# Gate and up projections with the weights standing and both halves of the activations in one moving operand; attention scores over zero-padded keys

## The chip, the cores and the metric

One Trainium2 chip, one core. The metric is the device time of one execution in microseconds (us); the shown time is a median of three runs. The profile is one execution on the same core.

## The reference

Two decoder layers over 256 tokens of width 1024, in fp32. Each layer is a feed-forward half step (FFN), a mixer (a state-space head group beside a windowed attention with 16 heads of 64) and a second FFN:

```python
def swiglu(x, w_gate, w_up, w_down):
    return (jax.nn.silu(x @ w_gate) * (x @ w_up)) @ w_down
...
for i in range(DEPTH):
    x = x + 0.5 * swiglu(rms_norm(x, ffn1_norm[i]), ffn1_w_gate[i], ffn1_w_up[i], ffn1_w_down[i])
    h = rms_norm(x, mix_norm[i])
    proj = h @ w_in[i]
...
    q = rms_norm(q.reshape(b, s, ATT_HEADS, ATT_HEAD_DIM), q_norm[i])
    k = rms_norm(k.reshape(b, s, ATT_HEADS, ATT_HEAD_DIM), k_norm[i])
    y_att = dilated_attention(q, k, v).reshape(b, s, ATT_WIDTH)
    x = x + jnp.concatenate([y_ssd, y_att], axis=-1) @ w_out[i]
    x = x + 0.5 * swiglu(rms_norm(x, ffn2_norm[i]), ffn2_w_gate[i], ffn2_w_up[i], ffn2_w_down[i])
```

Gate and up are 1024 x 2816 each, down is 2816 x 1024. The scores of a head are q times k over 64 values, with masks that are laid over them.

## The kernel before

A product of fp32 operands is made of three products of fp32r operands: each operand is split into a high part (a rounded copy, by ScalarE) and a low part (the operand less the copy, by VectorE), and `mm3` (L243) adds high x high, high x low and low x high in PSUM. Weights come from memory in halves of 128 x 1024, four staging buffers deep; `Stream.pump` (L161, L163) splits each half into one of nine slots (five of `hp`, four borrowed from `wk`), `take` hands a half to the matmuls and `done` gives its slot back. `tick()` stands after each group of matmuls: it lets the stream split what has a free slot and moves the spawned generators (transposes, heads and the like) one step, so that they are laid between the groups. Instructions run in order on each engine.

The normalised activations are held transposed, features on partitions, as a high tile and a low tile of 8 x 256 (`xT_tiles`).

In an FFN (`ffn`) the 2816 columns of gate and up go in 11 steps of 256 columns each. A step makes two PSUM tiles (one for each 128 tokens) of 512 columns, 256 of gate and 256 of up: the activations stand in the array (128 x 128) and the weights move (512 columns). That is 8 feature tiles x 2 token tiles x 3 = 48 matmuls of 512 columns, in eight groups of six. `gated` (L404, L405) then takes Silu of the gate's columns on ScalarE and multiplies by the up's columns on VectorE. The product has tokens on partitions, and the down projection wants features there: `rest` waits four ticks, transposes the four 128 x 128 blocks on TensorE (L399) and splits the result out of PSUM (L209, L210). The first step has its own loop (`unit_first`), since the second token tile is normalised late. The pool `ps` has four PSUM banks for all large products; the down projection (`project_out`) holds all four (`acc`).

In the mixer, `unit_ch` is a product with the weights standing and 256 activation columns moving, three loads and three matmuls for each pair of tiles (`pc`). For attention, `qk_norm_T` transposes q and k and writes each, 128 x 512 at a time, on ScalarE (L674); two heads share the 128 partitions. `head_pair` makes the scores of a head by two fp32 matmuls over its 64 partitions (256 and 128 columns; L689, L690, the profile shows each as two records), one head on the lower and one on the upper half of the array. Batches of four head pairs follow the q and k blocks that they need.

Of the kernel before, what the change touches and what calls it, by code (L numbers as in the profile page):

```python
# [50 lines left out]
def tile_hybrid_trunk(ctx: ExitStack, tc: tile.TileContext, x, w_ffn_in, w_ffn_down, w_z, w_dtz,  # L51
# [188 lines left out]
    def tok(t):  # L240
        return slice(t * 128, (t + 1) * 128)
# [19 lines left out]
            guard["act"], guard["vec"] = urgent(split)(xT[0][:, 4 * b:4 * b + 4, tok(t)], xT[1][:, 4 * b:4 * b + 4, tok(t)], p)  # L261

    def xT_tiles():
        return (big.tile([128, KT, 256], F32R, tag="xTh", name="xTh"),
                big.tile([128, KT, 256], F32R, tag="xTl", name="xTl"))

    @urgent
    def normed(t, wB, acc=None, scale=None):
# [22 lines left out]
    def mm_pair(name, n):  # L291

        return [ps.tile([128, 512], F32, tag="mm", name=f"{name}{i}")[:, :n] for i in range(2)]
# [28 lines left out]
    def unit_ch(xT, o):  # L322

        for a in range(2):
            hf = st.take()
            for i in range(2):
# [6 lines left out]
                    st.done(hf)  # L333
                tick()

    def project_out(nk, yT, tail, scale, norm, need=None):

        wB = None  # L340
        acc = [mm_pair(f"acc{t}", 512) for t in range(2)]

        def step(k, t, b, hf):
            n = slice(b * 512, (b + 1) * 512)
            yh, yl = [a[:, 0, tok(t)] for a in yT(k)]
            mm3(acc[t][b], yh, yl, hf[0][:, n], hf[1][:, n], k == 0, k == nk - 1)

        for k in range(0, nk - tail, 2):
            hf = [st.take(), st.take()] if k + 1 < nk - tail else [st.take()]
            if need:  # L350
                until(need(k + len(hf) - 1))
            for t in range(2):
                for i, h in enumerate(hf):
                    for b in range(2):
                        step(k + i, t, b, h)
                    if t:
                        st.done(h)
                    tick()
            if wB is None and k >= nk // 2 and norm is not None:
                wB = norm_weight(*norm)  # L360
        late = [(k, st.take()) for k in range(nk - tail, nk)]
        if need:
            until(need(nk - 1))
        st.hold = HOLD and norm is not None
        for b in range(2):
            for i, (k, h) in enumerate(late):
                step(k, 0, b, h)
                if i % 2:
                    tick()
        xT = xT_tiles() if wB is not None else None  # L370
        xn = normed(0, wB, acc, scale)
        for b in range(2):
            for i, (k, h) in enumerate(late):
                if b and i == tail - TR_POS and xT:
                    transpose_norm(0, xn, xT)
                step(k, 1, b, h)
                if b:
                    st.done(h)
                if i % 2:
                    tick()  # L380
        xn = normed(1, wB, acc, scale)
        st.hold = False
        return xT, xn


    def ffn(layer, f, xT, xn, norm, tail):
        hA = [big.tile([128, 16, 256], F32R, tag=f"yA{i}", name=f"hA{i}") for i in range(2)]
        hB = [big.tile([128, FT - 16, 256], F32R, tag=f"yB{i}", name=f"hB{i}") for i in range(2)]

        def hT(k, n=1):  # L390
            return [a[:, k:k + n, :] for a in hA] if k < 16 else [b[:, k - 16:k - 16 + n, :] for b in hB]

        def rest(j, h):

            yield 4
            p = pt.tile([128, 2, 256], F32, tag="tr", name="tr")
            for i in range(2):
                for t in range(2):
                    pe.transpose(p[:, i, tok(t)], h[:, t, i * 128:(i + 1) * 128], ident)  # L399
            split(*hT(2 * j, 2), p)  # L400

        def gated(p, sg, h, t):

            act.activation(sg[:, t, :], p[:, 0:256], AF.Silu)  # L404
            vec.tensor_tensor(h[:, t, :], sg[:, t, :], p[:, 256:512], op=OP.mult)  # L405

        for j in range(FF // 256):
            sg = wk.tile([128, 2, 256], F32, tag="t2", name="sg", bufs=5)
            h = wk.tile([128, 2, 256], F32, tag="t2", name="hh", bufs=5)
            p = mm_pair("pgu", 512)  # L410
            if j == 0:
                halves = [st.take() for _ in range(4)]
                for t in range(2):
                    if t:
                        transpose_norm(1, xn, xT)
                        if layer == 0 and f == 0:
                            small_params()
                    unit_first(512, xT, t, halves, p[t])
                    gated(p[t], sg, h, t)
            else:  # L420
                unit_tok(512, 2, xT, p)
                for t in range(2):
                    gated(p[t], sg, h, t)
            spawn(rest(j, h))
        return project_out(FT, hT, tail, 0.5, norm)


    def mixer(layer, xT, xn, norm, tail):
# [221 lines left out]


        qT = wk.tile([128, 8, 256], F32, tag="e0", name="qT", bufs=1)
        kT = wk.tile([128, 8, 256], F32, tag="e1", name="kT", bufs=1)
        vt = [wk.tile([128, D], F32, tag="xn", name=f"vt{t}") for t in range(2)]

        def qk_norm_T(which, b, pp, dst):
            ss = sm.tile([128, 2, 8], F32, tag="qss", name="qss")
            for t in range(2):
                sq = wk.tile([128, 8, E], F32, tag="t2", name="sq", bufs=5)
                act.activation(sq.rearrange("p h e -> p (h e)"), pp[t], AF.Square, scale=1.0 / 8)  # L660
                vec.tensor_reduce(ss[:, t, :], sq, axis=AX.X, op=OP.add)
            rr = rsqrt(ss, [128, 2, 8])
            qn = []
            for t in range(2):
                q = wk.tile([128, 8, E], F32, tag="t2", name="qn", bufs=5)
                vec.tensor_tensor(q, pp[t].rearrange("p (h e) -> p h e", e=E),
                                  rr[:, t, :, None].to_broadcast([128, 8, E]), op=OP.mult)
                qn.append(q.rearrange("p h e -> p (h e)"))
            yield 3
            for t in range(2):  # L670
                p = pt.tile([128, 4, 128], F32, tag="tr", name="tr")
                for i in range(4):
                    pe.transpose(p[:, i, :], qn[t][:, i * 128:(i + 1) * 128], ident)
                act.activation(dst[:, 4 * b:4 * b + 4, tok(t)], p, AF.Copy, scale=qkw[:, layer, which:which + 1])  # L674
            events.add(f"qk{which}{b}")

        RNG = (slice(0, 256), slice(256, 384))
# [1 line left out]
        def head_pair(pr):  # L679
# [4 lines left out]
            yield 1  # L684
            scs = []
            for i in range(2):
                o = slice(64 * i, 64 * i + 64)
                p = pt.tile([128, 384], F32, tag="s", name="psc")
                pe.matmul(p[:, 0:256], qT[o, pr, 128:256], kT[o, pr, :], start=True, stop=True)  # L689
                pe.matmul(p[:, 256:384], qT[o, pr, 0:128], kT[o, pr, 0:128], start=True, stop=True)  # L690
                sc = wk.tile([128, 384], F32, tag="sc", name="sc", bufs=4)
                nm = sm.tile([128, 2], F32, tag="nm", name="nm", bufs=4)
                den = sm.tile([128, 2], F32, tag="den", name="den", bufs=4)
                for j, c in enumerate(RNG):
                    vec.tensor_tensor_reduce(sc[:, c], p[:, c], amask[:, c], scale=-1.0, scalar=3e38,
                                             op0=OP.add, op1=OP.min, accum_out=nm[:, j:j + 1])
                for j, c in enumerate(RNG):
                    act.activation(sc[:, c], sc[:, c], AF.Exp, bias=nm[:, j:j + 1], scale=-1.0,
                                   accum_out=den[:, j:j + 1])
                vec.reciprocal(den, den)  # L700
                for j, c in enumerate(RNG):
                    vec.tensor_scalar(sc[:, c], sc[:, c], den[:, j:j + 1], None, op0=OP.mult)
                scs.append(sc)
                yield PAIR_LAG[i]
# [27 lines left out]
        for b, which in QKV_ORDER:  # L732
            pp = mm_pair("pq", 512)
            unit_tok(512, 2, xT, pp)
            if which < 2:
                spawn(qk_norm_T(which, b, pp, (qT, kT)[which]))
            else:
                for t in range(2):
                    act.copy(vt[t][:, 512 * b:512 * b + 512], pp[t])
                events.add(f"v{b}")  # L740
# [34 lines left out]
def _layout(inp):  # L775
# [2 lines left out]
    r = {"x": a["x"]}  # L778
    ffn_in = []
    for f in (1, 2):  # L780
        gu = [a[f"ffn{f}_w_{n}"].reshape(DEPTH, D, FF // 256, 256) for n in ("gate", "up")]
        ffn_in.append(_pack(np.stack(gu, axis=3).reshape(DEPTH, D, 2 * FF), 4, 512).transpose(0, 2, 1, 3, 4))
    r["w_ffn_in"] = np.stack(ffn_in, axis=1)
    r["w_ffn_down"] = np.stack([_pack(a[f"ffn{f}_w_down"], 2, 1024)[:, :, 0] for f in (1, 2)], axis=1)
    w = a["w_in"]
# [54 lines left out]
```

## Time and profile before

| what | value |
|---|---|
| median of three runs | 1246.6 us (1245.03 to 1246.91) |
| the profiled execution: time | 1244.8 us |
| its span, first to last instruction | 1242.9 us |
| granted TensorE clock, mean | 1.000 |
| TensorE matmul busy | 1228.6 us |
| VectorE busy | 784.7 us |
| ScalarE busy | 673.0 us |

The busy time of an engine is the time in which at least one of its instructions runs. The records of matmuls overlap each other, so that their mean duration is longer than the distance from one to the next. The chain is the work that ended last, followed back from the end; its pieces stand in order of time, with start and length, and their lengths add up.

### The profile page before, as it was taken

How to read it: one execution, taken by the hardware profiler on the slowest of the kernel's cores; microseconds unless marked ns; L12 is line 12 of the kernel's file. 1: busy time of each engine (PE TensorE's matmuls, PEld its weight loads, DVE VectorE, ACT ScalarE, POOL GpSimd, SP SyncE). 2: the span in 40 equal slices, each digit the busy share in tenths (PEclk: the TensorE clock that was granted, in tenths of full speed). 3: DMA queues.
4: the chain of work that ended last, by engine and by line, in shares of the span. 5: the costliest groups of instructions: out<-in, count | busy, mean ns of one | idle time of the engine just before them, and what ended most of it. 6: DMA issues, size and time to landing. Idle time of an engine off the chain costs nothing.

```text
span 1242.9 us, 16699 instructions
## 1 busy us (share of the span) xinstructions
PE 1228.6 (99%) x6176; PEld 1019.3 (82%) x6176; DVE 784.7 (63%) x1392; ACT 673.0 (54%) x1094; POOL 5.3 (0%) x13
## 2 busy tenths in 40 slices
PE   6999999999999999999999999999999999999998
PEld 5888888998777788888878888889987778888887
DVE  6655546897786576555466554478887865755541
ACT  5544434777866455444355443466778663644430
POOL 0000000000000000000000000000000000000000
PEclk9999999999999999999999999999999999999999
DMA  8755552654334557555447554645533443765550
GB/s 281 261 186 186 171 203 104 208 181 138 119 105 137 167 180 237 188 180 181 169 163 245 186 187 152 206 139 190 180 123 101 134 138 117 249 208 184 188 171 34
DMA packets 59409, 213.56 MB, mean 172 GB/s; under 512 B 6848, under 2 KB 7104, under 8 KB 59328
## 3 DMA queue, kind: packets, MB, share of 16 engines
q1 hardware_dynamic: 58176, 208.76, 49.7%
q0 software_dynamic: 1008, 3.67, 0.9%
q8 instruction: 49, 0.80, 0.3%
q14 instruction: 32, 0.26, 0.1%
q10 hardware_dynamic: 144, 0.07, 0.0%
HBM read 211.42 MB, written 1.05 MB: 171 GB/s over the span
## 4 chain that ended last, share of the span: by engine, by line
PE 97%; DVE 1%; DMA 1%; ACT 0%; issue 0%; SPq 0%; ACTq 0%
PE pgu L246 13%; PE pgu L245 13%; PE pgu L247 13%; PE acc L245 9%; PE acc L247 9%; PE acc L246 9%; PE pq L245 4%; PE pq L246 4%; PE pq L247 4%; PE pc L247 2%; PE pc L245 2%; PE pc L246 2%; PE psc L689 2%; PE tr L399 2%; PE pz L245 1%; PE pz L246 1%
## 5 line engine op out<-in xcount | busy, mean ns | idle before, releaser
L163 DVE TENSOR_TENSOR wl<-w,wh 128x1024 fp32r<-128x1024 f32 x268 | 327.6, 1224 | 191.6 <-ACT wh L161 189.0
L161 ACT CAST wh<-w 128x1024 fp32r<-128x1024 f32 x268 | 280.6, 1051 | 238.5 <-PE pgu L247 85.1
L163 DVE TENSOR_TENSOR we<-w,we 128x1024 fp32r<-128x1024 f32 x124 | 151.4, 1225 | 128.9 <-ACT we L161 127.6
L161 ACT CAST we<-w 128x1024 fp32r<-128x1024 f32 x124 | 130.2, 1053 | 136.5 <-PE pgu L247 68.9
L245 PE MATMUL pgu<-wh,xTh 128*128 128x512 f32 x392 | 156.8, 400 | 0.8 <-ACT xTh L209 0.8
L246 PE MATMUL pgu<-wl,xTh 128*128 128x512 f32 x392 | 154.6, 394 | 0.6 <-DVE wl L163 0.6
L247 PE MATMUL pgu<-wh,xTl 128*128 128x512 f32 x392 | 154.0, 394 | 0.0
L245 PE MATMUL pgu<-we,xTh 128*128 128x512 f32 x312 | 123.1, 395 | 0.0
L246 PE MATMUL pgu<-we,xTh 128*128 128x512 f32 x312 | 121.8, 390 | 0.0
L247 PE MATMUL pgu<-we,xTl 128*128 128x512 f32 x312 | 121.3, 390 | 0.0
L245 PEld LDWEIGHTS pgu<-wh,xTh 128*128 128x128 f32 x392 | 74.4, 190 | 17.0 <-ACT xTh L209 1.9
L246 PEld LDWEIGHTS pgu<-wl,xTh 128*128 128x128 f32 x392 | 74.5, 190 | 16.6 <-DVE wl L163 1.8
L247 PEld LDWEIGHTS pgu<-wh,xTl 128*128 128x128 f32 x392 | 74.4, 190 | 16.0 <-DVE xTl L210 0.3
L245 PE MATMUL pq<-wh,xTh 128*128 128x512 f32 x192 | 80.1, 417 | 0.0
L247 PE MATMUL pq<-wh,xTl 128*128 128x512 f32 x192 | 78.4, 408 | 0.0
L246 PE MATMUL pq<-wl,xTh 128*128 128x512 f32 x192 | 78.0, 406 | 0.0
L245 PE MATMUL pc<-xTh,wh 128*128 128x256 f32 x256 | 72.9, 285 | 0.0
L247 PE MATMUL pc<-xTh,wl 128*128 128x256 f32 x256 | 72.4, 283 | 0.0
L246 PE MATMUL pc<-xTl,wh 128*128 128x256 f32 x256 | 72.4, 283 | 0.0
L247 PEld LDWEIGHTS pgu<-we,xTl 128*128 128x128 f32 x312 | 58.5, 188 | 12.3
L246 PEld LDWEIGHTS pgu<-we,xTh 128*128 128x128 f32 x312 | 58.6, 188 | 12.1 <-DVE we L163 0.4
L245 PEld LDWEIGHTS pgu<-we,xTh 128*128 128x128 f32 x312 | 58.6, 188 | 11.9 <-ACT xTh L209 0.3
(189 smaller groups left out, 2222.2 us busy)
## 6 DMA issues: line engine op xcount, KB each, us to landing
w<-in_w_ffn_in_dram SPq DMA_DIRECT2D x176, 512.0 KB, 4.6
w<-in_w_ffn_down_dram SPq DMA_DIRECT2D x88, 512.0 KB, 3.7
w<-in_w_qkv_dram SPq DMA_DIRECT2D x48, 512.0 KB, 3.6
w<-in_w_xbc_dram SPq DMA_DIRECT2D x32, 512.0 KB, 4.4
w<-in_w_out_dram SPq DMA_DIRECT2D x32, 512.0 KB, 3.7
w<-in_w_z_dram SPq DMA_DIRECT2D x12, 512.0 KB, 4.7
nw<-in_norms_dram POOLq DMA_DIRECT2D x7, 512.0 KB, 4.2
w<-in_w_dtz_dram SPq DMA_DIRECT2D x4, 544.0 KB, 5.0
```

Of the source, the lines that this page charges most:

```text
L161: act.copy(h, src)
L163: vec.tensor_tensor(l, src, h.bitcast(F32), op=OP.subtract)
L245: pe.matmul(o, ah, bh, start=first, stop=False)
L246: pe.matmul(o, ah, bl, start=False, stop=False)
L247: pe.matmul(o, al, bh, start=False, stop=last)
L399: pe.transpose(p[:, i, tok(t)], h[:, t, i * 128:(i + 1) * 128], ident)
L689: pe.matmul(p[:, 0:256], qT[o, pr, 128:256], kT[o, pr, :], start=True, stop=True)
```

## The change

The steps 1 to 10 of each FFN hold the weights still. A step makes gate first (`pg`, two banks of 512 columns, one for each 128 features), then up (`pu`): for each weight tile one matmul of the high weights with the activations' high and low parts side by side (512 columns), and one of the low weights with the high activations (256 columns, into the first half of the bank). The two halves of a bank are added outside TensorE: ScalarE copies the second half out, VectorE adds the first. The product then has its features on partitions already, and is split straight into the down projection's operand. Step 0 stays as it was, with its transposes. The high and low activations lie in one tile, and the weights of steps 1 to 10 are laid out in memory in pieces of gate and of up.

The keys are kept twice as wide, each head's with zeros in the other head's 64 partitions: GpSimd sets the zeros once in each mixer, ScalarE writes k in two pieces of 64 partitions, and the scores are taken over all 128 partitions.

```diff
     def xT_tiles():
-        return (big.tile([128, KT, 256], F32R, tag="xTh", name="xTh"),
-                big.tile([128, KT, 256], F32R, tag="xTl", name="xTl"))
+        both = big.tile([128, KT, 2, 256], F32R, tag="xT", name="xT")
+        return both[:, :, 0, :], both[:, :, 1, :], both
...
+    def unit_ch_wide(xT, o):
+        for a in range(2):
+            hf = st.take()
+            for i in range(2):
+                for k in range(4):
+                    c = slice(k * 256 + 128 * i, k * 256 + 128 * i + 128)
+                    kk = 4 * a + k
+                    def wide(stop):
+                        pe.matmul(o[i], hf[0][:, c], xT[2][:, kk].rearrange("p s n -> p (s n)"),
+                                  start=kk == 0, stop=stop)
+                    if kk < KT - 1:
+                        wide(False)
+                    pe.matmul(o[i][:, 0:256], hf[1][:, c], xT[0][:, kk, :], start=False, stop=False)
+                    if kk == KT - 1:
+                        wide(True)
+                if i:
+                    st.done(hf)
+                tick()
...
-        def rest(j, h):
+        def turn(j, h):
...
+        def rest(j, h):
+            yield 1
+            split(*hT(2 * j, 2), h)
+
+        def halves_added(name, p):
+            o = wk.tile([128, 2, 256], F32, tag="t2", name=name, bufs=5)
+            for i in range(2):
+                act.copy(o[:, i, :], p[i][:, 256:512])
+                vec.tensor_tensor(o[:, i, :], p[i][:, 0:256], o[:, i, :], op=OP.add)
+            return o
...
+        spawn(turn(0, h))
+        for j in range(1, FF // 256):
+            pg, pu = mm_pair("pg", 512), mm_pair("pu", 512)
+            unit_ch_wide(xT, pg)
+            sg = halves_added("sg", pg)
+            act.activation(sg, sg, AF.Silu)
+            unit_ch_wide(xT, pu)
+            h = halves_added("hh", pu)
+            vec.tensor_tensor(h, sg, h, op=OP.mult)
             spawn(rest(j, h))
...
-        kT = wk.tile([128, 8, 256], F32, tag="e1", name="kT", bufs=1)
+        kz = wk.tile([128, 4, 2, 256], F32, tag="e1", name="kz", bufs=1)
+        pool.memset(kz[64:128, :, 0, :], 0.0)
+        pool.memset(kz[0:64, :, 1, :], 0.0)
...
-                act.activation(dst[:, 4 * b:4 * b + 4, tok(t)], p, AF.Copy, scale=qkw[:, layer, which:which + 1])
+                w = qkw[:, layer, which:which + 1]
+                if which:
+                    for i in range(2):
+                        o = slice(64 * i, 64 * i + 64)
+                        act.activation(kz[o, :, i, tok(t)], p[o], AF.Copy, scale=w[o])
+                else:
+                    act.activation(qT[:, 4 * b:4 * b + 4, tok(t)], p, AF.Copy, scale=w)
...
-                o = slice(64 * i, 64 * i + 64)
                 p = pt.tile([128, 384], F32, tag="s", name="psc")
-                pe.matmul(p[:, 0:256], qT[o, pr, 128:256], kT[o, pr, :], start=True, stop=True)
-                pe.matmul(p[:, 256:384], qT[o, pr, 0:128], kT[o, pr, 0:128], start=True, stop=True)
+                pe.matmul(p[:, 0:256], qT[:, pr, 128:256], kz[:, pr % 4, i, :], start=True, stop=True)
+                pe.matmul(p[:, 256:384], qT[:, pr, 0:128], kz[:, pr % 4, i, 0:128], start=True, stop=True)
```

## Rows read from the trace of the kernel before

**Rows 1.** The page, busy us, share of the span and instructions of each engine.
```profile
PE 1228.6 (99%) x6176; PEld 1019.3 (82%) x6176; DVE 784.7 (63%) x1392; ACT 673.0 (54%) x1094; POOL 5.3 (0%) x13
```
**Rows 2.** The page, shares of the chain that ended last, by engine.
```profile
PE 97%; DVE 1%; DMA 1%; ACT 0%; issue 0%; SPq 0%; ACTq 0%
```
**Rows 3.** Busy time by stretch, in steps of one FFN, 60 to 148 us.
```profile
core 0: us, PE busy (x) PEld busy (x) DVE busy (x) ACT busy (x) POOL busy (x), PEclk, DMA share, GB/s
60.00:148.00 88.00, 88.00 (x403) 72.91 (x402) 47.87 (x54) 42.48 (x55) 0.00 (x0) 1.00 0.54 185
```
**Rows 4.** The chain in order of time, one step of gate and up: start, us, what.
```profile
80.52 0.44 PE tr L399 x4
80.96 0.24 PE pgu L245
...
91.88 0.44 PE tr L399 x4
```
**Rows 5.** The page, costliest groups: count | busy us, mean ns | idle before.
```profile
L245 PE MATMUL pgu<-wh,xTh 128*128 128x512 f32 x392 | 156.8, 400 | 0.8 <-ACT xTh L209 0.8
```
**Rows 6.** The chain, weights standing, 256 columns moving: first and last of 67 pieces.
```profile
231.98 0.12 PE pc L245
...
239.90 0.12 PE pc L245
```
**Rows 7.** The chain at one head's scores, and the two matmuls behind.
```profile
385.32 0.63 PE psc L689 x2
385.94 0.22 PE psc L690 x2
386.17 0.43 PE acc L245
386.59 0.23 PE acc L246
```
**Rows 8.** The chain where two heads' scores stand together: first piece, and the matmul behind.
```profile
334.21 0.73 PE psc L689 x3
...
335.41 0.43 PE pq L245
```
**Rows 9.** The chain at fp32 matmuls over all 128 partitions, between fp32r ones.
```profile
286.54 0.43 PE pst L553 x2
286.97 0.23 PE pq L247
...
289.04 0.24 PE pcb L580 x2
...
298.21 0.84 PE py L595 x8
299.05 0.49 PE po L600 x2
```
**Rows 10.** Groups of instructions by line and shape, ScalarE and VectorE.
```profile
L674 ACT ACTIVATE kT<-tr,qkw 128x512 f32<-128x512 f32 x8 | 5.2, 680 | 0.0
L555 ACT COPY xB<-pst 128x256 f32<-128x256 f32 x8 | 3.0, 371 | 3.0 <-PE pst L553 3.0
...
L405 DVE TENSOR_TENSOR hh<-sg,pgu 128x256 f32<-128x256 f32 x88 | 36.1, 414 | 0.0
```
**Rows 11.** VectorE in order of time around a step's end in mid-FFN.
```profile
97.55 1.23 DVE L163 TENSOR_TENSOR wl<-w,wh 128x1024 fp32r<-128x1024 f32 x1 [1.17 <-ACT wh L161]
98.69 0.41 DVE L405 TENSOR_TENSOR hh<-sg,pgu 128x256 f32<-128x256 f32 x1
```
**Rows 12.** The chain near the third FFN's start: the transposes of its step 0.
```profile
647.35 0.44 PE tr L399 x4
```
**Rows 13.** VectorE in order of time: the two multiplications of that FFN's step 1.
```profile
656.41 0.75 DVE L405 TENSOR_TENSOR hh<-sg,pgu 128x256 f32<-128x256 f32 x2
```
**Rows 14.** Weight loads in order of time, scores of the second four pairs.
```profile
378.78 0.29 PEld L689 LDWEIGHTS psc<-kT,qT 64*128 64x128 f32 x2 [0.36 <-ACT kT L674]
```

More of the change, by code (lines that the diff above doesn't have):

```diff
@@ L405, in gated @@
             vec.tensor_tensor(h[:, t, :], sg[:, t, :], p[:, 256:512], op=OP.mult)
[L407 to L423, printed above, removed]
+        def rest(j, h):
[7 more added lines that the diff above has]
+            return o
+        sg = wk.tile([128, 2, 256], F32, tag="t2", name="sg", bufs=5)
+        h = wk.tile([128, 2, 256], F32, tag="t2", name="hh", bufs=5)
+        p = mm_pair("pgu", 512)
+        halves = [st.take() for _ in range(4)]
+        for t in range(2):
+            if t:
+                transpose_norm(1, xn, xT)
+                if layer == 0 and f == 0:
+                    small_params()
+            unit_first(512, xT, t, halves, p[t])
+            gated(p[t], sg, h, t)
+        spawn(turn(0, h))
[7 more added lines that the diff above has]
+            vec.tensor_tensor(h, sg, h, op=OP.mult)
             spawn(rest(j, h))
@@ L652, in mixer, with qk_norm_T @@
         qT = wk.tile([128, 8, 256], F32, tag="e0", name="qT", bufs=1)
-        kT = wk.tile([128, 8, 256], F32, tag="e1", name="kT", bufs=1)
+        kz = wk.tile([128, 4, 2, 256], F32, tag="e1", name="kz", bufs=1)
+        pool.memset(kz[64:128, :, 0, :], 0.0)
+        pool.memset(kz[0:64, :, 1, :], 0.0)
         vt = [wk.tile([128, D], F32, tag="xn", name=f"vt{t}") for t in range(2)]
-        def qk_norm_T(which, b, pp, dst):
+        def qk_norm_T(which, b, pp):
             ss = sm.tile([128, 2, 8], F32, tag="qss", name="qss")
@@ L735, in mixer @@
             if which < 2:
-                spawn(qk_norm_T(which, b, pp, (qT, kT)[which]))
+                spawn(qk_norm_T(which, b, pp))
             else:
@@ L780, in _layout @@
     for f in (1, 2):
-        gu = [a[f"ffn{f}_w_{n}"].reshape(DEPTH, D, FF // 256, 256) for n in ("gate", "up")]
-        ffn_in.append(_pack(np.stack(gu, axis=3).reshape(DEPTH, D, 2 * FF), 4, 512).transpose(0, 2, 1, 3, 4))
+        gu = [a[f"ffn{f}_w_{n}"] for n in ("gate", "up")]
+        first = _pack(np.concatenate([w[:, :, 0:256] for w in gu], axis=2), 4, 512).transpose(0, 2, 1, 3, 4)
+        rest = np.stack([_pack(w[:, :, 256:], 8, 256)[:, 0] for w in gu], axis=2)
+        ffn_in.append(np.concatenate([first, rest], axis=1))
     r["w_ffn_in"] = np.stack(ffn_in, axis=1)
```

## The prediction, on record before the result

> **What bounds the kernel now.** I read the busy times first [rows 1], then the chain by engine [rows 2]: TensorE is busy for 1228.6 of 1242.9 us and holds 97% of the chain. The stretch in the middle of an FFN [rows 3] says the same where the change lands: TensorE 88.00 of 88.00 us at a granted clock of 1.00 (the 2.4 GHz level), VectorE 54%, ScalarE 48%. So time comes out only by shortening TensorE's own sequence, and goes in wherever TensorE must wait for ScalarE, VectorE or a PSUM bank. The third view is the chain in order of time, which gives the distance from one matmul to the next; the recorded 400 ns of a 512-column matmul [rows 5] overlap their neighbours' and price nothing.
>
> **Gate and up.** One step runs from one set of transposes to the next: 91.88 - 80.52 = 11.36 us [rows 4]. The transposes take 0.44, the 48 matmuls 91.88 - 80.96 = 10.92, so 0.2275 each; 512 columns at 2.4 GHz are 0.2133, and 0.014 goes on top of each. The new step has 2 products x 2 banks x 8 weight tiles = 32 pairs of a 512 and a 256: the same 24,576 columns, 64 loads where the matmuls had 48. A 256-column matmul with a load of its own, weights standing, is in the trace: 66 distances from 231.98 to 239.90, 0.120 each [rows 6]. Sum: 32 x 0.2275 + 32 x 0.120 = 11.12 us. The 16 more matmuls cost 0.20, the transposes give back 0.44: 0.24 us a step, and 40 steps (10 in each of four FFNs) give **-9.6 us**. The margin is thin: 7.5 ns more for each pair takes it all. The trace has no alternation of 512 and 256. Below: nothing, since no row has a 256 under 0.120. Above: the load of the next weights must fit under 256 columns. The closest thing to a bare load is the fp32 matmul of 64 columns, 0.84 us for 8, 0.105 each [rows 9], which does fit in 0.120; wholly in the open it would be 0.105 a pair. I take zero, as the 256s of [rows 6] are nearest and hide their loads.
>
> **Scores.** A head's four records take 0.63 + 0.22 us, and the matmul behind them 0.43 where its follower takes 0.23: 1.05 us with the 0.20 behind [rows 7]. Over all 128 partitions, fp32 matmuls of the same width stand between the same neighbours: 0.43 and 0.49 for two records of 256 columns, with 0.23 for the next fp32r matmul, so nothing lost behind them; and 0.24 for two of 128 [rows 9]. So what the half array costs is 0.17 going in and 0.20 coming out. New: 0.46 + 0.22 = 0.68 (0.65 to 0.73), a saving of 0.37. Of 32 heads, 28 stand alone; once in each layer two stand together, 335.41 - 334.21 + 0.20 = 1.40 us [rows 8] against 1.36. Sum: 28 x 0.37 + 2 x 0.04 = **-10.5 us** (9 to 11.5).
>
> **Taking the sums out of PSUM.** Before, a step fills two banks in 11.36 us; now each product fills two in 16 x (0.2275 + 0.120) = 5.56 us, and the next but one needs them back: the first bank 5.56 us after the product's end, the second 1.39 later (its first matmul comes four pairs on), at 6.95. How late the engines are now: the transposes stand 30 matmuls behind a step's end, so the step before ended at 91.88 - 6.83 = 85.05, the next at 96.41; its last multiplication ended at 99.10, 2.7 us behind, after a weight half of 1.23 us that stood in front of it [rows 4, 11]. In the new order ScalarE makes two copies of 0.37 behind its weight half, VectorE two additions of 0.41 behind its own [rows 10]: both banks are back about 3.2 us after the end. Room: 2.4 us. The engines' load rises by 1.52 us a step on VectorE (two more of 0.41 and a product over 512 at about 0.69) to 69%, and by at most 1.5 on ScalarE (four copies of 0.37, Silu once over 512 in place of twice over 256) to 63% [rows 3, 10].
>
> At an FFN's start the weight stream refills its slots and both engines run late: step 0 ended at 647.35 - 6.83 = 640.52, step 1 at 651.88, its multiplications at 657.16, 5.3 us behind [rows 12, 13], the latest of the four FFNs. With 0.5 more for the additions, the banks come back at 5.4 and 5.8, just under 5.56 and 6.95. The second product then inherits the first one's Silu and additions. I take 0.5 us for each FFN, **+2 us** (0 to 16: up to 2 us at each of two products).
>
> **Keys.** GpSimd's zeros cost nothing: they have the whole stretch from the mixer's start over the z and xBC products to the first k write, and stand on that queue behind the issue of one row of norm weights alone; without that cover they would hold back the first scores only. ScalarE writes k twice at about 0.68 [rows 10], 0.68 more for each token tile. Most of it is hidden, since heads come ticks later; but at the second four pairs TensorE's load already waited 0.36 us for this write [rows 14], and two such writes are ahead of it: 0 to 1.4 us in each layer, I take 0.7, **+1.4 us**. The buffer holds four pairs, so the second k block's write must wait for the first four pairs' scores; in the chain these all stand ahead of the transposes of that block, so nothing waits for it.
>
> **Hidden or unchanged.** The weight stream has the same halves, sizes and order of use; the one activation tile makes the first matmul wait for the low part, which the third waits for anyway. The splitting of the product is moved, not added; it reads a buffer, not PSUM.
>
> **Sum.** 1244.8 - 9.6 - 10.5 + 2 + 1.4 = 1228.1 us for the profiled execution, which lies 1.8 under the median of the runs shown; against that median, **1230 us**.
>
> **Rivals.**
> *The loads come into the open* (other side). The next 512's load must hide under 256 columns. At 0.030 us a pair, 1280 pairs cost 38 us: 1268. It decides from 16.7 / 1280 = 13 ns a pair. Wholly in the open, 16 more loads than before in each of 40 steps, at 0.105, are 67 us: 1297. Against it: 0.120 for 256 with a load each [rows 6], and 0.105 for load and 64 columns [rows 9]. The Trainium skill (TensorE: Matmul & The Clock Gate, Part 3, The mechanism) says that a load overlaps matmuls in flight only where the row groups differ; by that, every load of a step would show, and the kernel would be slower. [Rows 6] don't bear that out: loads over all rows leave only 0.013 beyond the 0.107 of the columns. Chance 0.08.
> *PSUM comes back late at the FFNs' starts*: the upper bound, 2 us at two products of each FFN, +14 on the forecast: 1236 to 1246. For it: 5.3 of 5.56 us are used there [rows 13]. Chance 0.12.
> *PSUM comes back late in every step*: if two weight halves instead of one stand before the additions, 2.4 us are added to 3.2, which is over 5.56; beyond that each 0.5 us costs 0.5 x 80 products = 40: about 1270. Against it: one half is what [rows 11] show. Chance 0.04.
> *The scores keep their cost*, if it is fp32 and not the half array that costs: 1240.5. Against it [rows 9]. Chance 0.08.
> *More than forecast*: no stalls and the cheap ends, under 1223. Chance 0.04.
>
> **Numbers.** The forecast's own case (1223 to 1236) has 0.64. Less than 0.2%, 2.5 us, is about what a measurement of this kernel can't tell from no change. Faster: 0.64 + 0.08 + 0.04 + 0.09 of the late starts, 0.85; same 0.03 of the late starts and 0.01 of the loads, 0.04; slower 0.07 of the loads and 0.04, 0.11. The range leaves out the loads, every step late, and the cheap ends, 0.16: 1223 to 1244 us.
>
> **What would show it.** In the chain: a step of 11.12 us without transposes, pieces alternating at 0.23 and 0.12. If the small pieces read 0.15 or the large 0.25, the loads' rival holds. Scores at 0.68 with 0.23 behind them. Waits of TensorE, or chain pieces of ScalarE and VectorE, inside steps 1 and 2 of an FFN tell of late banks; in later steps, of the third rival. Above 1244 one of these has come in; under 1223 a pair costs less than its parts.

## The result, and the profile after

The changed kernel takes 1237.07 us (median of 4 runs, 1236.44 to 1238.98) against 1245.82 (1244.75 to 1246.91) for the kernel before beside it: ratio 0.9933, 95% interval 0.9921 to 0.9944, or 8.75 us less. Forecast were 1230 us and a range of 1223 to 1244: the direction and the range hold, the size is about half. The profiled execution took 1238.98 us, its span is 1237.2.

The page's busy times and the chain by engine, beside [rows 1, 2]:

```profile
PE 1218.3 (98%) x6656; PEld 1034.7 (84%) x6656; DVE 835.0 (67%) x1512; ACT 719.6 (58%) x1222; POOL 8.7 (1%) x17
...
PE 93%; DVE 2%; ACT 2%; DMA 2%; issue 1%; SPq 0%; DVEq 0%; ACTq 0%
```

TensorE's busy time fell by 10.3 us, the span by 5.7. Some 2 us of that gap lie at the execution's start: the transposes of the second token tile's activations, in the first FFN, start at 23.57 us against 21.30 before, and the chain's piece of a load of x there is 10.50 us long instead of 8.44; in the runs below the same start lies anywhere from 20.47 to 23.25. So the stages are compared without it, FFN 1 from those transposes on, the others from their normalised activations' first transpose, each to the next stage's:

| us | FFN 1 | mixer 1 | FFN 2 | FFN 3 | mixer 2 | FFN 4 |
|---|---|---|---|---|---|---|
| before | 179.33 | 236.90 | 187.66 | 187.69 | 236.89 | 193.07 |
| after | 178.66 | 234.89 | 187.06 | 187.09 | 233.49 | 192.45 |

An FFN gives 0.6 us where the forecast had 2.4 - 0.5; a mixer gives 2.0 and 3.4 where it had 5.25 - 0.7.

**Gate and up.** The chain in order of time, one product (start, us, what), beside [rows 4]:

```profile
81.94 0.23 PE pu L347
82.17 0.12 PE pu L352
82.28 0.23 PE pu L347
...
87.57 0.23 PE pg L347
```

No transposes, and pieces of 0.23 and 0.12 as the forecast wanted; only the lengths of whole products tell more. One takes 87.57 - 81.94 = 5.63 us, 0.352 for each of 16 pairs; 5.56 and 0.3475 were forecast. The same 5.63 stands in all four FFNs, and no piece of another engine lies inside. From one start to the next, large and small ones take 232 and 118 ns, 240 and 120, 236 and 114, and then the same again: a round of six matmuls, 1060 ns.

**PSUM.** VectorE in order of time at a product's end. The next `pu` starts two products behind 81.94 and ends at 98.84:

```profile
98.66 0.42 DVE L438 TENSOR_TENSOR hh<-pu,hh 128x256 f32<-128x256 f32 x1
99.96 1.23 DVE L163 TENSOR_TENSOR wl<-w,wh 128x1024 fp32r<-128x1024 f32 x1 [0.88 <-ACT wh L161]
101.10 0.42 DVE L438 TENSOR_TENSOR hh<-pu,hh 128x256 f32<-128x256 f32 x1
```

The second bank is back at 101.52, 2.7 us behind the end, after one weight half (3.2 was forecast, behind one half as well).

**Scores.** The chain at one head, beside [rows 7]:

```profile
385.37 0.43 PE psc L735 x2
385.81 0.22 PE psc L736 x2
386.03 0.23 PE acc L245
386.26 0.23 PE acc L246
```

0.65 us and nothing behind it, where it was 0.63 + 0.22 + 0.20: 0.40 saved for a head that stands alone.

**Waits.** All of TensorE's waits, grouped (who waited, on whom: us in total, times, longest):

```profile
PE tr L260 <- DVE xn L288: 11.4, 4, 10.7
PE po L765 <- ACT pT L759: 1.1, 2, 0.7
PE psc L735 <- DVE yT L210: 0.8, 1, 0.8
PE pgu L246 <- DVE wl L163: 0.6, 1, 0.6
PE psc L735 <- ACT kz L719: 0.3, 2, 0.2
PE pgu L245 <- ACT xT L209: 0.2, 1, 0.2
```

The first row is almost all of it the execution's start (10.7 us, 8.0 before). The two `pgu` rows are step 0 of an FFN, as before. The other three rows stand in the mixers, 2.2 us in all, and the kernel before has none of them. In order of time the first mixer's are these, on TensorE:

```profile
382.12 0.70 PE L735 MATMUL psc<-kz,qT 128*128 128x256 f32 x2 [0.17 <-ACT kz L719]
...
405.87 0.70 PE L735 MATMUL psc<-kz,qT 128*128 128x256 f32 x2 [0.77 <-DVE yT L210]
...
411.75 0.65 PE L765 MATMUL po<-pT,vt 128*64 128x256 f32 x2 [0.74 <-ACT pT L759]
```

and on ScalarE, ahead of the first, the doubled k writes at one go:

```profile
379.98 2.80 ACT L719 ACTIVATE kz<-tr,qkw 64x512 f32<-64x512 f32 x4
```

**Step 0.** TensorE's weight loads have a wait that the kernel before lacks at this place: in step 0 of each FFN the load for a matmul with the activations' low part waits 0.4 to 0.5 us for VectorE to write that part. In FFN 2 the chain leaves TensorE there; in the kernel before it stays:

```profile
445.72 1.14 DVE we L163
446.86 0.61 DVE xT L210
447.47 0.04 issue
447.51 0.50 PE pgu L247
```

From the matmul ahead of it to the one behind it 0.81 us pass where two matmuls take 0.45: 0.35 more (0.28 in FFN 1), 1.3 us in the four FFNs. The high and the low part share one tile now, and these matmuls also stand in another order than before; no run parts the two.

### The profile page after: what moved, and what is told of

It is laid out like the page before. It is cut to its first block, busy times and chain, and to the rows that moved or that the text cites. A ratio compares the mean times of both kernels' runs of the same rounds, so it can differ in the third digit from the quotient of the medians.

```text
span 1237.2 us, 17952 instructions
## 1 busy us (share of the span) xinstructions
PE 1218.3 (98%) x6656; PEld 1034.7 (84%) x6656; DVE 835.0 (67%) x1512; ACT 719.6 (58%) x1222; POOL 8.7 (1%) x17
## 4 chain that ended last, share of the span: by engine, by line
PE 93%; DVE 2%; ACT 2%; DMA 2%; issue 1%; SPq 0%; DVEq 0%; ACTq 0%
PE pu L347 12%; PE pg L347 12%; PE acc L247 8%; PE acc L245 8%; PE acc L246 8%; PE pu L352 6%; PE pg L352 6%; PE pq L245 4%; PE pq L247 4%; PE pq L246 4%; PE pc L247 2%; PE pc L246 2%; PE pc L245 2%; PE pz L245 1%; PE pz L246 1%; PE pz L247 1%
## 5 line engine op out<-in xcount | busy, mean ns | idle before, releaser
L347 PE MATMUL pu<-xT,wh 128*128 128x512 f32 x360 | 127.7, 398 | 0.0
L347 PE MATMUL pg<-xT,wh 128*128 128x512 f32 x360 | 127.1, 397 | 0.0
L347 PE MATMUL pu<-xT,we 128*128 128x512 f32 x280 | 99.1, 397 | 0.0
L347 PE MATMUL pg<-xT,we 128*128 128x512 f32 x280 | 99.0, 397 | 0.0
L352 PE MATMUL pu<-xT,wl 128*128 128x256 f32 x360 | 93.8, 281 | 0.0
L352 PE MATMUL pg<-xT,wl 128*128 128x256 f32 x360 | 93.4, 280 | 0.0
L245 PE MATMUL pq<-wh,xT 128*128 128x512 f32 x192 | 79.1, 412 | 0.0
L247 PE MATMUL pq<-wh,xT 128*128 128x512 f32 x192 | 77.6, 404 | 0.0
L246 PE MATMUL pq<-wl,xT 128*128 128x512 f32 x192 | 77.2, 402 | 0.0
L352 PE MATMUL pg<-xT,we 128*128 128x256 f32 x280 | 73.0, 280 | 0.0
L245 PE MATMUL pc<-xT,wh 128*128 128x256 f32 x256 | 72.9, 285 | 0.0
L246 PE MATMUL pc<-xT,wh 128*128 128x256 f32 x256 | 72.4, 283 | 0.0
```

Of the source, the lines that this page charges most:

```text
L245: pe.matmul(o, ah, bh, start=first, stop=False)
L246: pe.matmul(o, ah, bl, start=False, stop=False)
L247: pe.matmul(o, al, bh, start=False, stop=last)
L347: pe.matmul(o[i], hf[0][:, c], xT[2][:, kk].rearrange("p s n -> p (s n)"), start=kk == 0, stop=stop)
L352: pe.matmul(o[i][:, 0:256], hf[1][:, c], xT[0][:, kk, :], start=False, stop=False)
```

## The experiments

Two questions were open: why a pair costs 0.352, and where the scores' gain went. For the first, theory A blames the order (a large and a small matmul in turn), theory B the roles (the weights stand and the activations move, not the other way round). For the second, the loss may be the keys' own (M1) or come from gate and up beside them (M2).

**Half of the order undone.** In each bank four large matmuls, then four small ones; in the second half of the features the small ones first.

```diff
+                for k in range(4 if a == 0 else 0):
+                    wide(k)
+                for k in range(4):
+                    low(k)
+                for k in range(4 if a else 0):
+                    wide(k)
```

> The changed kernel with the order inside a group of gate and up turned: four matmuls of 512 in a row, then four of 256 (in the second half of a product the 256s first). Nothing else changes, neither columns nor loads. Theory A (alternation: a 512 is dearer where it follows a 256, since its load has only the 256's time): three of four 512s fall from 0.234 to 0.227, about 5 ns for each of 1280 pairs, 6.5 us less than the changed kernel, a product at 5.55 us. Theory B (roles: a 512 with the weights standing and the activations moving costs 0.234 whatever stands before it): no change within 1 us, a product stays at 5.63.

Measured: 1235.27 us, ratio 0.9925 (0.9911 to 0.9939). The chain, one product:

```profile
80.03 0.93 PE pu L345 x4
80.95 0.47 PE pu L350 x4
...
82.35 0.96 PE pu L350 x8
...
85.64 0.93 PE pg L345 x4
```

A product takes 5.61 us, between the two expectations: order matters, but four in a row at 0.2325 are not the 0.2275 of before. The kernel before has such a beginning too. In its first mixer, the 512s that follow 256s (the chain; five distances from 216.40 to 217.56, five more to 218.69) take 0.232 first and 0.226 from the sixth on:

```profile
216.28 0.12 PE pz L247
216.40 0.23 PE pz L245
...
217.56 0.23 PE pz L247
...
218.69 0.23 PE pz L246
```

Four in a row never come to the sixth.

**The keys alone**, on the kernel before:

```diff
-                pe.matmul(p[:, 0:256], qT[o, pr, 128:256], kT[o, pr, :], start=True, stop=True)
+                pe.matmul(p[:, 0:256], qT[:, pr, 128:256], kz[:, pr % 4, i, :], start=True, stop=True)
```

> The kernel before with the zero-padded keys alone. Theory M1 (the scores give back some 11 us, and the doubled write of k and what it shifts in the mixer take about half of it): 5.4 us less than before, each mixer 2 to 3.5 us shorter, with waits at the scores behind the second k block. Theory M2 (the mixer's waits come from the weight stream as the new gate and up leave it): 9 us less or more, no new waits.

Measured: 1239.94 us, ratio 0.9965 (0.9952 to 0.9977), 5.05 less. The mixers take 234.11 and 234.33 (236.90 before), the FFNs what they took. The mixers fall short with gate and up untouched.

**Gate and up alone**, the changed kernel with k and scores as before:

```diff
-                pe.matmul(p[:, 0:256], qT[:, pr, 128:256], kz[:, pr % 4, i, :], start=True, stop=True)
+                pe.matmul(p[:, 0:256], qT[o, pr, 128:256], kT[o, pr, :], start=True, stop=True)
```

> The changed kernel with the keys as before: gate and up alone. If the parts add up: 2.4 us less than before (0.6 in each FFN), mixers as before to 0.3 us. If the new gate and up disturb the mixer's weight stream (M2): the mixers are longer than before by 2 us or more, and the whole is no faster.

Measured: 1242.53 us, ratio 0.9982 (0.9974 to 0.9991), 2.46 less. Mixers 236.91 and 236.89, FFNs 187.06. The two parts add up: -5.05 - 2.46 = -7.5, inside the interval of the whole change (-7.0 to -9.8). M2 is out.

**Small matmuls in the order of before.** In the kernel before, the second of the three matmuls is parted into two of 256 columns.

```diff
+                        pe.matmul(o[t][:, 0:256], xT[1][:, kk, tok(t)], hf[0][:, m[0]], start=False, stop=False)
+                        pe.matmul(o[t][:, 256:512], xT[1][:, kk, tok(t)], hf[0][:, m[1]], start=False, stop=False)
```

> The kernel before, activations standing, with the third product of each three (low activations) parted in two matmuls of 256, so that half of its 512s follow a 256 and half a 512; 16 more matmuls and loads in each step, about 0.012 to 0.014 each, 8 to 9 us in all. Theory A: the 512s behind a 256 take 0.234, those behind a 512 0.227; 40 x 16 x 7 ns = 4.5 us on top. Theory B: both 0.227.

Measured: 1256.4 us (one execution). The chain:

```profile
83.82 0.23 PE pgu L318
84.05 0.11 PE pgu L319
84.17 0.12 PE pgu L320
84.28 0.23 PE pgu L321
84.52 0.24 PE pgu L318
```

A step takes 11.597 us, not 11.354: 0.243 for 16 more matmuls, 15.2 ns each. Two small ones side by side between large ones cost about what any extra matmul costs; there is no penalty of a mixed order as such.

**The roles, large matmuls only.** The small ones are left out; in FFN 1 the weights stand and the activations move, in FFN 2 activations take both parts, in FFN 3 weights, in FFN 4 the activations stand and the weights move.

```diff
+                    stand = hf[0][:, c] if form[0] == "w" else xT[0][:, kk, 128 * i:128 * i + 128]
+                    move = acts if form[1] == "x" else hf[k % 2][:, 512 * i:512 * i + 512]
+                    pe.matmul(o[i], stand, move, start=kk == 0, stop=kk == KT - 1)
```

> The changed kernel with the 256-column matmuls left out of gate and up (the output lacks those terms), and in each of the four FFNs another choice of what stands and what moves in the 512s: first FFN weights stand and activations move, second activations stand and activations move, third weights stand and weights move, fourth activations stand and weights move. A product is 16 matmuls of 512 with nothing between. Theory A (alternation): 0.227 in all four, 3.64 us a product. Theory B (roles): 0.231 to 0.234 where the weights stand and the activations move, 3.70 to 3.74, and 0.227 in the fourth; the second and third say whether it is what stands or what moves that costs.

Measured: 1126.62 us (one execution). Most products are longer here, since TensorE waits at them (the median is 3.75 to 4.07 us); where nothing keeps it waiting, a product takes 16 x 0.227 = 3.63 us, in each of the four FFNs. Roles don't matter for the large ones; theory B falls.

**The two writes of k on two engines**, in the changed kernel:

```diff
-                    for i in range(2):
-                        o = slice(64 * i, 64 * i + 64)
-                        act.activation(kz[o, :, i, tok(t)], p[o], AF.Copy, scale=w[o])
+                    act.activation(kz[0:64, :, 0, tok(t)], p[0:64], AF.Copy, scale=w[0:64])
+                    vec.tensor_scalar(kz[64:128, :, 1, tok(t)], p[64:128], w[64:128], None, op0=OP.mult)
```

> The changed kernel with one of the two pieces of k written by VectorE (from PSUM, with the weight as a scalar) in place of ScalarE. If ScalarE's doubled writes are what makes the mixers give back: the wait at the scores behind the second k block goes and each mixer is 1 to 1.5 us shorter, 2 to 3 us in all. If the late waits come from the weight stream of the out projection: 1 us or less in all.

Measured: 1235.59 us, ratio 0.9916 (0.9903 to 0.9928). That interval overlaps the changed kernel's; the stages are clearer: mixers 233.57 and 232.54, 1.3 and 0.95 less. Of the mixers' waits one group is left (TensorE's waits):

```profile
PE po L764 <- ACT pT L758: 1.6, 3, 0.8
```

The waits for `kz` and for `yT` are gone. The wait for `kz` is in every run with both writes on ScalarE and in none of the five with the writes split. The wait for `yT`, which the profile puts down to VectorE, goes with ScalarE's load as well: of the split runs only the last one below, where ScalarE copies three times over, has it (0.2 us).

**Both together**, four by four and k on two engines:

```diff
+                for k in range(4 if a == 0 else 0):
+                    wide(k)
...
+                    vec.tensor_scalar(kz[64:128, :, 1, tok(t)], p[64:128], w[64:128], None, op0=OP.mult)
```

> The grouped order and the split writes of k together. If they add up: 1.2 us (grouping) and 1 to 3 us (split) less than the changed kernel, 1232 to 1235 us.

Measured: 1233.72 us, ratio 0.9906 (0.9891 to 0.9921); mixers 232.75 and 232.31, an FFN 186.73 where the changed kernel takes 187.06. By stages, the two gains stand side by side.

**What the small matmul is.** FFN 1: the small ones too have 512 columns, 14 of them in a product; FFN 2: both with the high weights, 14 small; FFN 3: small ones into PSUM banks of their own, 16; FFN 4: the activations stand, 14 small.

```diff
+                    if form == "full":
+                        if kk < KT - 1:
+                            pe.matmul(o[i], hf[1][:, c], acts, start=False, stop=False)
+                    elif form == "bank":
+                        pe.matmul(own[i][:, 0:256], hf[1][:, c], xT[0][:, kk, :], start=kk == 0, stop=kk == KT - 1)
```

> What in the mix of 512s and 256s costs the 4.4 ns a pair, one variant in each FFN (the outputs lack or garble the small terms). First FFN: the small matmul is a 512 as well (low weights, both halves of the activations): 0.455 a pair if alternating two weight tiles costs nothing, 0.459 or more if that is the cause. Second: the small one takes the high weights, so that only one weight tile is read: 0.3475 if the second tile is the cause, 0.352 if not. Third: the small ones in PSUM banks of their own: 0.3475 if writing half of the bank between two whole writes is the cause, 0.352 if not. Fourth: the same alternation with the activations standing and the weights moving: 0.3475 if the alternation costs only where weights stand, 0.352 if the alternation of sizes by itself is the cause.

Measured: 1253.74 us (one execution). Where nothing keeps TensorE waiting, a product takes 6.80 us (30 matmuls, 0.2267 each), 5.333, 5.65 and 5.333, in the order of the FFNs. The fast ones are those with 14 small matmuls, so this run mixed two things up, and the next keeps them apart.

**Fourteen or sixteen.** FFN 1: as in the change with the last small matmul of each bank left out, 14; the others with all 16: both with the high weights, the activations standing, both with the low weights.

```diff
+                    skip = form == "both14" and last
+                    pe.matmul(o[i], hf[big_w][:, c], acts, start=kk == 0, stop=skip)
+                    if not skip:
+                        pe.matmul(o[i][:, 0:256], hf[small_w][:, c], xT[0][:, kk, :], start=False, stop=last)
```

> The run before this one had two differences at once in its second and fourth FFN (one weight tile, or activations standing; and the last small matmul of each bank left out, 14 for 16). Here they are parted, one variant in each FFN, the output garbled or lacking small terms. First: high and low weights as in the changed kernel, 14 small ones: 5.32 us a product if the count was the cause, 5.39 if not. Second: high weights in both, 16 small ones: 5.57 if reading one weight tile is what saves, 5.63 if not. Third: activations standing, 16 small ones: 5.57 if it is what stands, 5.63 if not. Fourth: low weights in both, 16 small ones: as the second.

Measured: 1232.73 us (one execution). The chain, first a product with 14 small ones (from 98.75 to 104.08), then one with 16 (from 501.51 to 507.16):

```profile
98.75 0.24 PE pu L354
98.98 0.12 PE pu L356
99.10 0.23 PE pu L354
...
102.57 0.46 PE pu L354 x2
...
104.08 0.24 PE pg L354
...
501.51 0.23 PE pg L354
501.75 0.12 PE pg L356
...
507.16 0.24 PE pu L354
```

With 14, ten pairs take 102.57 - 99.10 = 3.47 us, 0.347 each: the forecast's price of a pair. With 16 in unbroken turn, 5.65 = 16 x 0.353, whatever stands, moves or is loaded. (The changed kernel turns its last pair round in each bank, so two small ones meet, and it stands at 5.633.) So neither tile, nor bank, nor roles, but the order.

**Which order.** All of the work, with k on two engines: FFN 1 in turn, with the last small matmul of the first bank put off to the end of the product; FFN 2 two large, two small; FFN 3 in turn, but the fourth pair of each four turned round; FFN 4 the first bank's and second bank's large ones early, the small ones of the first features late.

```diff
+        "late": ("W0 L0 W1 L1 W2 L2 W3 L3", "W0 L0 W1 L1 W2 L2 W3 L3",
+                 "W4 L4 W5 L5 W6 L6 W7", "W4 L4 W5 L5 W6 L6 W7 L7 M7"),
+        "twos": ("W0 W1 L0 L1 W2 W3 L2 L3", "W0 W1 L0 L1 W2 W3 L2 L3",
...
+        "ends": ("W0 L0 W1 L1 W2 L2 L3 W3", "W0 L0 W1 L1 W2 L2 L3 W3",
...
+        "all": ("W0 W1 W2 W3", "W0 W1 W2 W3",
+                "W4 W5 W6 W7 M0 M1 M2 M3 L4 L5 L6 L7", "W4 W5 W6 W7 M0 M1 M2 M3 L4 L5 L6 L7"),
```

> The full work, with the split writes of k, and in each FFN another order of the same 16 large (W) and 16 small (L) matmuls of a product. Theory A2 (a strict one-to-one alternation falls into a slow rhythm of 0.353 a pair, and two Ws in succession set it back to 0.347, as the variant with 14 small ones showed): first FFN, W and L in turn with the left-over L's at the product's end, two Ws in succession once in a product: 5.56 to 5.58 us. Second, W W L L: 5.56 if two Ws are all it needs, 5.61 or more if two Ls in succession cost as much. Third, each group W L W L W L L W: two Ws meet at every group's end, 5.57 if it holds, and like the changed kernel, 5.63, if the two Ls spoil it. Fourth, eight Ws, then eight more with the Ls behind them: 5.60, near the grouped run's 5.61. If the rhythm isn't it, all four lie at 5.61 to 5.65.

Measured: 1234.93 us (one execution); products of 5.647, 5.573, 5.653 and 5.573 in this order. One pair of large matmuls in a row isn't enough where two small ones meet as well (first and third). Two by two gives 0.3483 a pair, which is 14.2 ns for each matmul over its columns at 2.4 GHz (213.3 and 106.7 ns).

**Two by two everywhere**, with k on two engines:

```diff
+                for k in (0, 2):
+                    for kk in (4 * a + k, 4 * a + k + 1):
...
+                        pe.matmul(o[i], hf[0][:, c], xT[2][:, kk].rearrange("p s n -> p (s n)"),
+                                  start=kk == 0, stop=False)
+                    for kk in (4 * a + k, 4 * a + k + 1):
...
+                        pe.matmul(o[i][:, 0:256], hf[1][:, c], xT[0][:, kk, :], start=False, stop=kk == KT - 1)
```

> The changed kernel with the split writes of k and, in all four FFNs, two large matmuls and then two small ones by turns. From the run of orders, 5.573 us a product against 5.633: 80 x 0.060 = 4.8 us less than the run with the split writes alone (1235.6), so 1230 to 1232 us. If the rhythm's cost only moves elsewhere: 1235.

Measured: 1231.28 us (1230.37 to 1232.18), ratio 0.9887 (0.9870 to 0.9903), 14.0 us less than before. The chain, one product:

```profile
80.80 0.46 PE pu L345 x2
81.26 0.23 PE pu L349 x2
...
86.37 0.46 PE pg L345 x2
```

86.37 - 80.80 = 5.57 us; an FFN takes 185.95, 1.7 less than before, and the mixers 233.42 and 232.86.

**How much room PSUM has.** The same, with each copy out of PSUM done three times:

```diff
+                for _ in range(3):
+                    act.copy(o[:, i, :], p[i][:, 256:512])
```

> The same kernel with each copy out of PSUM made three times over by ScalarE (the same values to the same place, full work otherwise): 0.74 us more before each addition, 1.5 us more a product, to ask how much room the banks have. If the room is what the prediction read (the banks come back about 2.7 to 3.2 us behind a product's end and are wanted at 5.56): within 1 us of the run beside it. If the room is smaller, or ScalarE's load (up to some 90%) breaks the weight stream: each 0.1 us late at every product costs 8 us.

Measured: 1232.61 us, ratio 0.9897 (0.9882 to 0.9912). The stretch of [rows 3] in this kernel:

```profile
60.00:148.00 88.00, 88.00 (x499) 76.47 (x498) 60.94 (x81) 74.82 (x143) 0.00 (x0) 1.00 0.61 193
```

ScalarE is busy for 85% of it, and TensorE still for all of it: a product stays at 5.573. Only early products of FFN 2 and FFN 3 grow, to 5.619, 5.661 and 5.867. So the banks' room is there in the steady steps, and an FFN's start is where it is smallest, as the forecast had it.

## Why the prediction was right in direction and off in size

**What bounds the kernel** was read rightly. ScalarE and VectorE got 47 and 50 us of work. TensorE's own waits grew by 4.3 us: 2.7 at the execution's start and 2.2 in the mixers, less 0.6 in the FFNs' steps 0. The measured time lies inside the range, but by luck: the forecast put 1236 to 1246 down to late banks at the FFNs' starts, which didn't come, and other losses, below, brought the time there.

**The pair of a 512 and a 256: the largest miss.** The prediction gave the mixture nothing: "I take zero, as the 256s of [rows 6] are nearest and hide their loads". In the changed order a pair takes 0.352 us, 4.6 ns over the 0.3475; 1280 pairs make 5.9 us of the 9.6. Ten steps of 11.354 were 113.54, so the products give 4 x (113.54 - 20 x 5.633) = 3.5 in the four FFNs, and the stages 2.5. The prediction named the weak point itself ("the trace has no alternation of 512 and 256", "7.5 ns more for each pair takes it all"), but kept its range for this cost at the loads' rival. A 512 from the middle of a row of 512s and a 256 from a row of 256s don't add up to their alternation. The trace of before had a nearer price: a 512 among the first five behind 256s, 0.232, which with 0.120 makes 0.352. That this beginning of a row is the same effect as the slower round is not shown. Shown: the extra goes away with the order alone (5.573 us a product two by two), and doesn't depend on what is loaded, what moves or which bank is written. Open: why the strict turn runs in this slower round, and why one large pair in a row restores it only where no two small ones meet.

**The loads' rival** didn't decide: the price is above the sum by 4.6 of the 13 ns that it would have needed. Nor does the number of loads set it, since the two-by-two order has the same 32 in a product; that a part of a load shows in one order and not in another is not excluded. The Trainium skill (TensorE: Matmul & The Clock Gate, Part 3, The mechanism) says that loads overlap matmuls in flight only where the row groups differ, and by that sentence every one of these would show, since all lie over the same rows; the same section also lets a load into the background weight buffer go ahead. At 14.2 ns over its columns for each matmul with its load, the runs fit the second and not the first.

**Late banks.** The 2 us for the FFNs' starts didn't come: no wait of TensorE inside steps 1 to 10, and triple copies bring 0.05 to 0.3 us at those very products. The working (3.2 of 5.56 us, one weight half in front) holds: 2.7.

**Step 0, a term put at nothing.** The forecast let the first matmul wait for the low part, "which the third waits for anyway", and counted no time. Measured are the 1.3 us above: 3.5 - 1.3 = 2.2, where the stages show 2.5. The run with gate and up alone has these waits, the run with the keys alone has not.

**Scores.** 0.65 against 0.68, nothing behind. With the heads placed as in the kernel before, that is an estimate of 28 x 0.40 + 2 x 0.03 = 11.3 us, against 10.5. What the half array cost was the way in and out, as [rows 9] said. The Trainium skill (TensorEngine Tiling (Array Packing), Key Properties) says that a change of tiling mode drains TensorE; the trace agrees, with 0.43 for the next matmul behind 64 rows [rows 7] and 0.23 behind 128.

**The k writes: mis-sized.** The prediction took 0.7 us a layer. The two mixers lost 11.3 - 5.4 = 5.9 us of the scores' gain, not 1.4. On two engines the same writes give 2.3 back, and the waits for `kz` and `yT` go. This doesn't rest on one pair of profiles: the two mixers together take 467.8 to 469.2 us in the six runs with both writes on ScalarE, and 465.1 to 466.3 in the five with the writes split. The forecast looked at the first scores behind the writes alone; it didn't follow ScalarE's delay to the later ticks.

Of the 3.6 us that are still lost with the writes split, 1.6 are TensorE's waits for `pT` of ScalarE. That a softmax is no longer covered by the shorter scores is likely, but not shown. Another 0.85 us stands where those waits hardly show. `po` of two heads runs side by side in the kernel before, 0.81 us for both up to the matmul behind, in order of time on TensorE:

```profile
418.86 0.66 PE L719 MATMUL po<-pT,vt 128*64 128x256 f32 x4
...
419.67 0.50 PE L245 MATMUL acc<-we,yT 128*128 128x512 f32 x1
```

With the writes split, the last two heads of the first mixer go one behind the other, since the second waits for its `pT`: 1.83 us, 0.17 of them that wait.

```profile
415.58 0.65 PE L764 MATMUL po<-pT,vt 128*64 128x256 f32 x2
...
416.62 0.65 PE L764 MATMUL po<-pT,vt 128*64 128x256 f32 x2 [0.17 <-ACT pT L758]
...
417.41 0.50 PE L245 MATMUL acc<-we,yT 128*128 128x512 f32 x1
```

About 1.1 us remain that no run here explains.

**GpSimd's zeros** cost nothing, as said: the page has 3.4 us more for them, and no wait of TensorE is on them.

## What to carry to other kernels

Price a new stream of matmuls from a row with the same order of sizes, not from the middle of rows of one size; where there is none, look at the first matmuls behind a change of size and keep a few nanoseconds a matmul in the range. In this kernel, matmuls of two sizes were faster in twos than in turn. When an engine's work is doubled inside a pipeline of queues laid out by hand, follow the delay to everything that it writes later, and try the other engine for half of it: here that was worth 2.3 us. A wait recorded as 0.17 us can cost 1.0 where it parts two things that ran side by side. What a change of shape costs is looked for behind the instruction too: 0.20 of the 0.40 us a head were on the next matmul's row.

## What the hardware did that was not expected

A 512 and a 256 in strict turn run at 0.353 us a pair over all 320 pairs of an FFN, in lengths that repeat (232/118, 240/120, 236/114 ns), while the same matmuls two by two run at 0.3483, and at 0.347 where one small one in eight is missing. Four large ones behind small ones take 0.2325 each, in a stream of large ones alone 0.227; in the kernel before, the first five 512s behind 256s take 0.232 and the next ones 0.226. Two heads' `po` of 64 columns each take 0.81 us together, one alone 0.79. None of these runs shows what sets the round.
